# Layer 0's output projection: a third buffer for the cast weights, the squares of h one unit later, gating split at the group change, the last two heads tile by tile

## The chip, the cores and the metric

The kernel runs on one core of a Trainium2 chip. The metric is the device time of one execution in microseconds (us). A profile is one further execution, recorded by the hardware; its rows name engine, source line (L952 is line 952 of the kernel), operation and tiles. The engines are PE (matrix products and transposes), DVE (vector), ACT (scalar functions and casts), POOL (GpSimd) and SP, whose queue issues nearly all transfers between HBM and SBUF. Each engine works through its own queue in order, and waits there for semaphores of the others.

## What is computed

A backbone of two layers over 512 latent and 256 context tokens of width 1024. Layer 0 is a gated DeltaNet in both directions with 16 value heads; layer 1 is grouped-query attention. What matters here is the end of layer 0 and the norm at the start of layer 1:

```python
def finish(o, z):                      # layer 0
    b, h, l, dv = o.shape
    o = rms_norm(jnp.transpose(o, (0, 2, 1, 3)), o_norm_g).astype(z.dtype)
    return (o.reshape(b, l, DN_VAL_DIM) * jax.nn.silu(z)) @ w_out
...
h_lat = h_lat + gate[:, None] * y_lat
h_ctx = h_ctx + gate_c * y_ctx
...
u_lat = rms_norm(h_lat, norm_g[i]) * (1.0 + scale[:, None]) + shift[:, None]   # layer 1
u_ctx = rms_norm(h_ctx, norm_g[i]) * (1.0 + scale_c) + shift_c
```

So the output projection multiplies a 768 x 2048 matrix by w_out (2048 x 1024); its result is gated and added to h, whose rows are then normalised, scaled and shifted for layer 1.

## The kernel before

**Products in float32 by halves.** Each factor is split into a rounded high part and the rest (fp32r each), and a product is three passes over PE: high x high, high x low, low x high (`PASS`, L1009). A weight row block of a head is loaded as `wo` (L942, three buffers), cast to its high part `woh` on ACT (`out_high`, L948 to L953, two buffers), and its low part `wol` is made half on POOL, half on DVE (`out_low`, L955 to L964, two buffers). The activations' halves `y` are made the same way (`out_second`, L1000 to L1007): cast on ACT (L1005), low part on DVE (L1006).

**Units.** The six token tiles lie in two groups of three (`GROUPS`, L970): first the two context tiles 0 and 1 and the latent tile 5, then the tiles 4, 3 and 2. A unit is one head of one group; units 0 to 15 are group 0, units 16 to 31 group 1. The loop over units n starts at L1340. In it stand, in this order:

- the loads of unit n+3 on SP's queue (`out_z`, `out_load`), and at some units loads of h, the gates or layer 1's key and value weights (`w1kv`, L1387, which share the three buffers of `wo`);
- `out_first(n + 2)`: three transposes on PE (L993) and three products with z on DVE (L996);
- from unit 24 on `u_first` (L1307): two transposes (L1312) of the normalised context tiles, scaled and shifted on DVE (L1314), for layer 1. Transposes of both kinds share a PSUM tile with two buffers (`ptr`, tag `tr`);
- `out_second(n + 2)` and `out_high(n + 2)`;
- from unit 24 on `u_second` (L1317): the halves `uC`, cast on ACT (L1320), low part on DVE (L1321);
- `chores`: small pieces of reciprocal square roots on DVE, which use a free part of unit n+2's PSUM tile; `norm_pieces(0)`, the norm of the first group's h, starts at unit 19;
- `out_low(n + 2)`;
- at units 21, 22 and 23 `normed` on ACT (L1301), one tile of the first group each;
- `products0(n)`: 18 products on PE, six for each of the three tiles (L1018), into six PSUM banks (`acc`) that sum over the 16 heads;
- after unit 15 and after unit 31 `gated` (L1243): six products of the banks with the gate on DVE (L1250), into the tiles `gy` in SBUF;
- at units 16, 17 and 18 two calls of `added` (L1254): the sum h + gy on POOL (L1257), the square of h with its row sum on ACT (L1258), and, for latent tiles, the write-out of h on SP's queue (L1260). For group 1 the six calls come after the loop, with the sum on DVE.

The order of PE, DVE, ACT and POOL is as written (`manual_schedule`, L1329); that of SP's queue is worked out by the scheduler. What writes a buffer waits until the last reader of the tile that had it before is done.

After the loop PE does the key and value products of the context tiles (`kv_block(k, (0, 1))`, L1516), while DVE makes the norm of group 1 (`norms1`, L1518) and ACT and DVE scale its tiles (`normed`, L1520); then the latent tiles are transposed and multiplied (L1522 to L1536).

Of the kernel before, what the change touches and what calls it, by code (L numbers as in the profile page):

```python
# [8 lines left out]
F32 = mybir.dt.float32  # L9
F32R = mybir.dt.float32r  # L10
I32 = mybir.dt.int32
AF = mybir.ActivationFunctionType
# [5 lines left out]
P = 128  # L18
D = 1024
# [4 lines left out]
QH, VH = 8, 16  # L24
# [73 lines left out]
def backbone(tc, a, out):  # L98
    nc = tc.nc
    V, S, G, T = nc.vector, nc.scalar, nc.gpsimd, nc.tensor  # L100
# [838 lines left out]
    def out_load(n):  # L939

        gi, h = units0[n]
        w = fw.tile([P, D], F32, tag="w", name=f"wo{h}_{gi}", bufs=3)  # L942
        w_at[n] = dma(w, a["dn_w_out"][0, h * P:(h + 1) * P, :]).ins
        loaded[n] = w
# [3 lines left out]
    def out_high(n):  # L948

        gi, h = units0[n]  # L950
        wh = fw.tile([P, D], F32R, tag="wh", name=f"woh{h}_{gi}")
        S.copy(wh, loaded[n])  # L952
        halves_w[n] = wh  # L953

# [12 lines left out]
    fw = fw_c.__enter__()  # L967


    GROUPS = (((0, 0, 192), (1, 64, 64), (5, 256, 64)), ((4, 128, 64), (3, 64, 192), (2, 0, 320)))  # L970
    ZCOLS = (((0, 256), (NCTX + 192, 128)), ((NCTX, 192), (NCTX + 320, 192)))
    units0 = [(gi, h) for gi in range(2) for h in range(VH)]
    ys, weights, zs, w_at, loaded = {}, {}, {}, {}, {}

    def out_z(n):

        gi, h = units0[n]
        z = fw.tile([P, 3 * P], F32, tag="z", name=f"z{h}_{gi}", bufs=3)
        c = 0
        for c0, m in ZCOLS[gi]:  # L980
            dma(z[:, c:c + m], z_d[h, :, c0:c0 + m])
            c += m
        zs[n] = z
# [3 lines left out]
    def out_first(n):  # L987

        gi, h = units0[n]
        z = zs.pop(n)  # L990
        pt = ptr.tile([P, 4, P], F32, tag="tr", name=f"pt{h}_{gi}")
        for j, (t, off, st_) in enumerate(GROUPS[gi]):
            T.transpose(pt[:, j, :], O[t][:, h, :], ident)  # L993
        for j, (t, off, st_) in enumerate(GROUPS[gi]):
            pj = pt[:, j].rearrange("p (a k) -> p a k", a=2)
            V.scalar_tensor_tensor(pj, pj, og, raw(z, off, [[st_, 2], [1, 64]]), ALU.mult, ALU.mult)  # L996
        begun[n] = pt
        return pt
# [12 lines left out]
    def products0(n, acc, js):  # L1011

        gi, h = units0[n]
        y, ww = ys[n], weights[n]
        for j in js:
            for nh in range(2):
                for x, (i, k) in enumerate(PASS):
                    T.matmul(acc[j][nh], y[i][:, j, :], ww[k][:, nh * 512:(nh + 1) * 512], start=h == 0 and x == 0, stop=h == VH - 1 and x == 2)  # L1018
# [6 lines left out]
    def first_acc(gi):  # L1025

        x = pU.tile([P, 2, 512], F32, tag="su", name=f"po{gi}0")
        return [x[:, nh] for nh in range(2)]

    with tc.tile_pool(name="psC", bufs=2, space=PSUM, reuse_waits="tile") as pcx:  # L1030
# [152 lines left out]
        chores = [(24, scale_pieces(0, 2)), (39, scale_pieces(5, 1))]  # L1183
# [40 lines left out]
    hpool = hpool_c.__enter__()  # L1224
    h_t = [hpool.tile([P, D], F32, tag=f"h{t}", name=f"h{t}") for t in range(NT)]
# [5 lines left out]
    hsq = hpool.tile([P, NT, 2], F32, tag="hsq", name="hsq")  # L1231
# [8 lines left out]

    ORDER = [t for g_ in GROUPS for t, _, _ in g_]

    def gated(gi, acc):  # L1243

        out_ = []
        for j, (t, _, _) in enumerate(GROUPS[gi]):
            for nh in range(2):
                gy = hpool.tile([P, 512], F32, tag="gy", name=f"gy{t}_{nh}", bufs=6)
                c = slice(nh * 512, (nh + 1) * 512)
                V.tensor_tensor(gy, acc[j][nh], gate0[:, 1 if t < 2 else 0, c], ALU.mult)  # L1250
                out_.append((t, nh, gy))
        return out_

    def added(t, nh, gy, E):  # L1254

        c = slice(nh * 512, (nh + 1) * 512)
        E.tensor_tensor(h_t[t][:, c], h_t[t][:, c], gy, ALU.add)  # L1257
        S.activation(gy, h_t[t][:, c], AF.Square, accum_out=hsq[:, ORDER.index(t), nh:nh + 1])  # L1258
        if t >= 2 and nh == 1:
            dma(h_d[t - 2], h_t[t])  # L1260

# [16 lines left out]
    def norm_pieces(gi):  # L1278

        r = hr[:, 3 * gi:3 * gi + 3]  # L1280
        y = hpool.tile([P, 3], F32, tag="hy", name=f"hy{gi}")
        sp = (yield)[:, 0:3]
        V.tensor_copy(sp, hsq[:, 3 * gi:3 * gi + 3, 0])
        V.tensor_tensor(sp, sp, hsq[:, 3 * gi:3 * gi + 3, 1], ALU.add)
        V.tensor_scalar(sp, sp, 1.0 / D, EPS, ALU.mult, ALU.add)
        V.tensor_copy(r, sp)
        V.tensor_single_scalar(sp.bitcast(I32), sp.bitcast(I32), 1, ALU.logical_shift_right)
        V.tensor_scalar(y.bitcast(I32), sp.bitcast(I32), -1.0, float(0x5F3759DF), ALU.mult, ALU.add)
        for i in range(3):
            room_ = yield  # L1290
            sp, t_ = room_[:, 0:3], room_[:, 64:67]
            V.tensor_copy(sp, y)
            V.scalar_tensor_tensor(t_, sp, -0.5, y, ALU.mult, ALU.mult)
            V.tensor_tensor(t_, t_, r, ALU.mult)
            V.scalar_tensor_tensor(r if i == 2 else y, t_, 1.5, y, ALU.add, ALU.mult)

    def normed(t, E):

        r = hr[:, ORDER.index(t):ORDER.index(t) + 1]
        if E is S:  # L1300
            S.activation(h_t[t], h_t[t], AF.Copy, scale=r)  # L1301
        else:
            E.tensor_scalar(h_t[t], h_t[t], r, None, ALU.mult)
# [3 lines left out]
    def u_first(k, j, tiles):  # L1307

        n = len(tiles) * P
        ps = ptr.tile([P, 4, P], F32, tag="tr", name=f"ht{k}_{j}")  # L1310
        for q, t in enumerate(tiles):
            T.transpose(ps[:, q, :], h_t[t][:, k * P:(k + 1) * P], ident)  # L1312
        pv = ps.rearrange("p a b -> p (a b)")[:, 0:n]
        V.tensor_scalar(pv, pv, au[1][:, j, 1, k:k + 1], au[1][:, j, 0, k:k + 1], ALU.mult, ALU.add)  # L1314
        turned_u[k, j] = pv
# [17 lines left out]
    chores = {4: scale_pieces(4, 1), 7: scale_pieces(3, 1), 10: scale_pieces(2, 1)}  # L1333
    for g_ in chores.values():
        next(g_)
    chores[19] = norm_pieces(0)
    squares = [(t, h) for t in (4, 3, 2) for h in range(VH)]
    late_adds = []
    loads0 = {3: lambda: load_h(0), 5: lambda: load_h(1), 7: lambda: load_h(5), 9: lambda: dma(gate0[:, 0], gate_d[0][:, 0]), 11: lambda: dma(gate0[:, 1], gate_d[0][:, 1]), 13: lambda: load_h(4), 18: lambda: load_h(3), 20: lambda: load_h(2)}
    for n in range(len(units0)):  # L1340
        gi, h = units0[n]
        if h == 0:
            acc = [acc0 if gi == 0 else first_acc(1)] + [[pf.tile([P, 512], F32, tag=f"po{j}{nh}", name=f"po{gi}{j}{nh}") for nh in range(2)] for j in (1, 2)]
        if n + 3 < len(units0):
            out_z(n + 3)
            out_load(n + 3)
        if n in loads0:
            with tc.issue_after(w_at[n + 3]):
                loads0[n]()
        more = n + 2 < len(units0)  # L1350
        pt = out_first(n + 2) if more else None
        if n >= 24:
            u_first(n - 24, 1, (0, 1))
        if more:
            out_second(n + 2)
            out_high(n + 2)
        if n >= 24:
            u_second(n - 24, 1, uC)
        if n == 19:
            next(chores[19])  # L1360
        for x in [x for x in chores if x <= n]:
            for _ in range(2):
                try:
                    chores[x].send(pt[:, 3])
                except StopIteration:
                    chores.pop(x)
                    break
        if more:
            out_low(n + 2)
        for t, h_ in squares[:5]:  # L1370
            square_o(t, h_)
        squares = squares[5:]
        scale_o(2 if n >= 12 else 1)
        if n in (21, 22, 23):
            normed(ORDER[n - 21], S)
        products0(n, acc, (1, 2) if n < 2 else (0, 1, 2))
        if h == VH - 1:
            late_adds = gated(gi, acc)
        if n in (16, 17, 18):
            for x in range(2):  # L1380
                added(*late_adds.pop(0), G)
        if gi == 1 and h in (4, 6, 8, 10):
            S.copy(wkv[0][:, k0:k0 + 2], wv)
            G.tensor_tensor(wkv[1][:, k0:k0 + 2], wv, wkv[0][:, k0:k0 + 2], ALU.subtract)
        if gi == 1 and h in (3, 5, 7, 9):
            k0 = h - 3
            w = fw.tile([P, D], F32, tag="w", name=f"w1kv_{k0}", bufs=3)  # L1387
            wv = w.rearrange("p (k n) -> p k n", n=512)
            dma(wv, wa[:, k0:k0 + 2, 1024:1536])
    for t, nh, gy in late_adds:  # L1390
        added(t, nh, gy, V)
    opool_x = [fw_c, opool_c, gates_c]
    for p_ in opool_x:
        p_.__exit__(None, None, None)
# [400 lines left out]
    with tc.tile_pool(name="fo", bufs=2, side="right", reuse_waits="tile") as f2, tc.tile_pool(name="psO", bufs=1, space=PSUM, reuse_waits="tile") as pO:  # L1795
# [4 lines left out]
        acc = [pg]  # L1800
# [4 lines left out]
        for t in range(4):  # L1805
            hs = f2.tile([P, D], F32, tag="hs", name=f"hs{t}")
            dma(hs, h_d[t])
            jk = f2.tile([P, D], F32, tag="jko", name=f"jko{t}")
# [3 lines left out]
            for nh in range(2):  # L1812
                c = slice(nh * 512, nh * 512 + 512)
# [11 lines left out]
            for hf in range(2):  # L1825
                c = t if hf == 0 else 7 - t
# [35 lines left out]
```

## Time and profile before

| | us |
|---|---|
| median of 3 runs | 1247.38 (1246.32 to 1249.12) |
| the profiled execution | 1246.04 |
| its span in the profile | 1244.3 |
| PE busy | 1151.5 (93%) |
| DVE, ACT, POOL busy | 827.8, 724.5, 599.3 |
| L1018, the projection's products, first to last start | 778.2 to 940.9 |

The profile is a page of sums and a trace of single instructions. A row of the trace's timeline has the start in us from the span's start, the busy time, the engine, the line, the operation with output and input tiles, a count, and in brackets the idle time of the engine before it and what ended that. A row of the waits has who waited for whom, the total in us, how often and the longest. A row of the windows has the busy time of each engine in a stretch, the share of its full clock that PE was granted (1.00 is full speed), and how busy the 16 DMA engines were. Products on PE are pipelined: the next starts before the one before it ends, so starts tell the rate.

### The profile page before, as it was taken

Reading aid. Unit: us, or ns where it says so; the run is one execution under the profiler, and the core shown is the slowest. Engines: PE = TensorE matmul, PEld = TensorE weight load, DVE = VectorE, ACT = ScalarE, POOL = GpSimd, SP = SyncE. Lnnn points to the kernel's source line nnn. Section 1 sums busy time; section 2 is a strip of 40 time slices with the busy share of each in tenths; the row PEclk is TensorE's granted clock in tenths of the full one; section 3 lists DMA queues with packets and bytes.
Section 4 is the critical chain, followed back from the end, with each engine's and each line's share of the span. In section 5 each row is a group of like instructions: output and inputs, shape, how many; then the busy total and the mean of one; then the engine's idle time right before and its main releaser. Section 6 shows DMA issues by size and latency. Waiting matters only on the chain. (4 is left out here: it accounts for less than half of the span.)

```text
span 1244.3 us, 28131 instructions
## 1 busy us (share of the span) xinstructions
PE 1151.5 (93%) x10755; PEld 926.9 (74%) x10755; DVE 827.8 (67%) x1865; ACT 724.5 (58%) x1934; POOL 599.3 (48%) x486
## 2 busy tenths in 40 slices
PE   4999999999789979899999999999879889999896
PEld 1776778888678867788666666887667779989784
DVE  2497666768688555575688988675556766556545
ACT  5543336665575767974689897543523246666631
POOL 0121133159998999700485598456534043140540
PEclk9999999999899989899999999999999999999998
DMA  9578965556425588655979765675634012111133
GB/s 322 176 216 263 299 221 162 137 151 183 136 83 159 181 253 261 191 193 184 274 215 241 237 172 143 199 224 153 213 103 136 18 41 62 35 34 52 51 110 93
DMA packets 165496, 204.56 MB, mean 164 GB/s; under 512 B 13393, under 2 KB 114930, under 8 KB 164594
## 3 DMA queue, kind: packets, MB, share of 16 engines
q1 hardware_dynamic: 146162, 193.10, 51.0%
q10 hardware_dynamic: 19200, 9.67, 2.6%
q8 instruction: 85, 1.39, 0.5%
q14 instruction: 49, 0.40, 0.1%
HBM read 161.96 MB, written 40.67 MB: 163 GB/s over the span
## 5 line engine op out<-in xcount | busy, mean ns | idle before, releaser
L1113 POOL TENSOR_TENSOR S<-S,glb 128x512 f32<-128x512 f32 x88 | 90.0, 1045 | 109.4 <-PE ks L1105 109.4
L1018 PE MATMUL po<-woh,y 128*128 128x512 f32 x384 | 128.7, 403 | 2.9 <-DVE gy L1250 2.9
L414 PE MATMUL g_v<-uh,wh 128*128 128x512 f32 (+1 forms) x256 | 91.4, 357 | 15.0 <-DVE sil_v L441 15.0
L755 POOL TENSOR_TENSOR X<-X,tmp 128x62 f32<-128x62 f32 (+15 forms) x93 | 95.7, 1029 | 6.5
L436 DVE SCALAR_TENSOR_TENSOR acc_v<-g_v,cwv,acc_v 128x510 f32<-128x510 f32 (+3 forms) x128 | 74.5, 609 | 34.5 <-ACT acc_v L433 33.0
L414 PE MATMUL g_z<-uh,wh 128*128 128x512 f32 (+1 forms) x256 | 88.4, 345 | 7.7 <-DVE sil_v L441 7.7
L1105 PE MATMUL ks<-S,ckq 128*64 128x256 f32 x768 | 93.5, 385 | 0.7 <-ACT O L1110 0.6
L754 POOL TENSOR_TENSOR tmp<-L,X 128x62 f32<-128x62 f32 (+15 forms) x93 | 89.9, 966 | 6.9
L414 PE MATMUL g_v<-ul,wh 128*128 128x512 f32 (+1 forms) x256 | 89.5, 350 | 0.0
L414 PE MATMUL g_v<-uh,wl 128*128 128x512 f32 (+1 forms) x256 | 88.9, 347 | 0.0
L961 POOL TENSOR_TENSOR wol<-wo,woh 128x512 fp32r<-128x512 f32 (+1 forms) x32 | 50.3, 1572 | 77.3 <-ACT woh L952 59.0
L414 PE MATMUL g_z<-ul,wh 128*128 128x512 f32 (+1 forms) x256 | 86.9, 340 | 0.0
L414 PE MATMUL g_z<-uh,wl 128*128 128x512 f32 (+1 forms) x256 | 86.9, 340 | 0.0
L1018 PEld LDWEIGHTS po<-woh,y 128*128 128x128 f32 x384 | 72.9, 190 | 18.2 <-issue 3.2
L1105 PEld LDWEIGHTS ks<-S,ckq 128*64 128x64 f32 x768 | 50.7, 136 | 39.7 <-ACT O L1110 9.9
L1018 PE MATMUL po<-wol,y 128*128 128x512 f32 x192 | 75.9, 396 | 1.5 <-POOL wol L961 1.4
L414 PEld LDWEIGHTS g_v<-uh,wh 128*128 128x128 f32 x256 | 50.6, 198 | 21.7 <-DVE sil_v L441 15.8
L211 POOL TENSOR_TENSOR wl_k<-w_k,wh_k 128x1024 fp32r<-128x1024 f32 x8 | 19.2, 2400 | 98.7 <-ACT wh_k L210 98.7
L1658 DVE TENSOR_TENSOR pT<-pt,pT 128x384 fp32r<-128x384 f32 x64 | 33.3, 554 | 42.2 <-ACT pT L1657 42.2
L1178 DVE TENSOR_TENSOR S<-su,S 128x512 f32<-128x512 f32 x88 | 56.6, 685 | 5.0 <-PE su L1160 3.4
L1108 DVE SCALAR_TENSOR_TENSOR r<-ks,negV,cv 128x128 f32<-128x128 f32 x192 | 56.6, 344 | 4.3 <-PE ks L1105 3.5
L414 PEld LDWEIGHTS g_z<-uh,wh 128*128 128x128 f32 x256 | 48.8, 191 | 13.6 <-DVE sil_v L441 8.5
(410 smaller groups left out, 3376.8 us busy)
## 6 DMA issues: line engine op xcount, KB each, us to landing
aw<-in_ada_w SPq DMA_DIRECT2D x24, 1024.0 KB, 7.8
w<-in_dn_w_in SPq DMA_DIRECT2D x40, 512.0 KB, 4.3
wo<-in_dn_w_out SPq DMA_DIRECT2D x32, 512.0 KB, 3.7
cv<-v_d SPq DMA_DIRECT2D x80, 128.0 KB, 5.5
df<-gc_d SPq DMA_DIRECT2D x48, 128.0 KB, 2.9
z_d<-zs SPq DMA_DIRECT2D x16, 384.0 KB, 4.9
v_d<-vt ACTq DMA_DIRECT2D x16, 384.0 KB, 3.8
t_d<-Tt SPq DMA_DIRECT2D x6, 1024.0 KB, 5.1
```

The source lines that it names most:

```text
L211: split_at[0] = E.tensor_tensor(wl[:, :, :m], w[:, :, :m], wh[:, :, :m], ALU.subtract).ins
L414: mm = T.matmul(pg_[:m, :n], w[:, k, :m], u[:, k, c0:c0 + n], start=k == 0 and n_ == 0, stop=k == KT - 1 and n_ == 2)
L436: V.scalar_tensor_tensor(acc[:, c0 + lo:c0 + hi], ps[:, lo + j - 2:hi + j - 2], cwv[:, j, ct:ct + 1], acc[:, c0 + lo:c0 + hi], ALU.mult, A ...
L754: E.tensor_tensor(tv, bcast(L[:, :, j + 1:, j], 3, j + 1), bcast(X[:, :, j, 0:j + 1], 2, n), ALU.mult)
L755: E.tensor_tensor(X[:, :, j + 1:, 0:j + 1], X[:, :, j + 1:, 0:j + 1], tv, ALU.subtract)
L961: G.tensor_tensor(wl[:, :c], w[:, :c], wh[:, :c], ALU.subtract)
L1018: T.matmul(acc[j][nh], y[i][:, j, :], ww[k][:, nh * 512:(nh + 1) * 512], start=h == 0 and x == 0, stop=h == VH - 1 and x == 2)
L1105: T.matmul(ks[r0:r0 + 64, w], kq[:, w, slot(hh), r0:r0 + 64], St[hh][:, d], start=True, stop=True)
L1108: V.scalar_tensor_tensor(r[:, 2 * j + i], ks[:, 0, i], negV[:, visit, t, h0 + i:h0 + i + 1], v[:, 2 * hh + i], ALU.mult, ALU.add)
L1113: G.tensor_tensor(St[hh], St[hh], bcast(g_, 3, P), ALU.mult)
L1178: V.tensor_tensor(St[hh], raw(sj, 0, [[512 - 1024 * j, 2], [P, 2], [1, P]]), St[hh], ALU.add)
L1658: V.tensor_tensor(lo, ps[:, :3], hi, ALU.subtract)
```

## The change

Four things in the loop over the units:

1. `woh` gets a third buffer (`bufs=3`).
2. At units 16 to 18 the squares of h are no longer issued with the sums; each pair is issued one unit later, on ACT behind that unit's casts of y and of the weights. The write-out of tile 5 goes with its square. `norm_pieces(0)` starts at unit 20 and `normed` runs at units 22, 23 and 24, one later than before.
3. At unit 15 the products are issued ahead of `out_second`, and the gating products of the first two tiles right behind them; those of the third tile follow `out_second` and `out_high`, ahead of `out_low`.
4. Units 30 and 31 are multiplied tile by tile: both heads of the first tile in unit 30, both heads of the second and then of the third tile in unit 31. The second group's gating writes its product in place, into the PSUM banks, and each tile is gated, added and squared before the next.

```diff
@@ out_high
-        wh = fw.tile([P, D], F32R, tag="wh", name=f"woh{h}_{gi}")
+        wh = fw.tile([P, D], F32R, tag="wh", name=f"woh{h}_{gi}", bufs=3)
@@ gated
-    def gated(gi, acc):
+    def gated(gi, acc, js):
 
         out_ = []
-        for j, (t, _, _) in enumerate(GROUPS[gi]):
+        for j in js:
+            t = GROUPS[gi][j][0]
             for nh in range(2):
-                gy = hpool.tile([P, 512], F32, tag="gy", name=f"gy{t}_{nh}", bufs=6)
                 c = slice(nh * 512, (nh + 1) * 512)
+                gy = acc[j][nh]
+                if gi == 0:
+                    gy = hpool.tile([P, 512], F32, tag="gy", name=f"gy{t}_{nh}", bufs=6)
                 V.tensor_tensor(gy, acc[j][nh], gate0[:, 1 if t < 2 else 0, c], ALU.mult)
@@ added
         E.tensor_tensor(h_t[t][:, c], h_t[t][:, c], gy, ALU.add)
-        S.activation(gy, h_t[t][:, c], AF.Square, accum_out=hsq[:, ORDER.index(t), nh:nh + 1])
+
+    def square_h(t, nh):
+
+        c = slice(nh * 512, (nh + 1) * 512)
+        jk = hpool.tile([P, 512], F32, tag="gy", name=f"jh{t}_{nh}", bufs=6)
+        S.activation(jk, h_t[t][:, c], AF.Square, accum_out=hsq[:, ORDER.index(t), nh:nh + 1])
         if t >= 2 and nh == 1:
             dma(h_d[t - 2], h_t[t])
@@ before the loop
-    chores[19] = norm_pieces(0)
+    chores[20] = norm_pieces(0)
+    late_squares = []
@@ in the loop
+        if n == VH - 1:
+            products0(n, acc, (0, 1, 2))
+            late_adds = gated(gi, acc, (0, 1))
         if more:
             out_second(n + 2)
             out_high(n + 2)
         if n >= 24:
             u_second(n - 24, 1, uC)
-        if n == 19:
-            next(chores[19])
+        if n == VH - 1:
+            late_adds += gated(gi, acc, (2,))
+        if n == 20:
+            next(chores[20])
...
-        if n in (21, 22, 23):
-            normed(ORDER[n - 21], S)
-        products0(n, acc, (1, 2) if n < 2 else (0, 1, 2))
-        if h == VH - 1:
-            late_adds = gated(gi, acc)
+        for t, nh in late_squares:
+            square_h(t, nh)
+        late_squares = []
+        if n in (22, 23, 24):
+            normed(ORDER[n - 22], S)
+        last = len(units0) - 1
+        if n >= last - 1:
+            for j in ((0,), (1, 2))[n - last + 1]:
+                products0(last - 1, acc, (j,))
+                products0(last, acc, (j,))
+        elif n != VH - 1:
+            products0(n, acc, (1, 2) if n < 2 else (0, 1, 2))
         if n in (16, 17, 18):
             for x in range(2):
+                late_squares.append(late_adds[0][:2])
                 added(*late_adds.pop(0), G)
@@ after the loop
-    for t, nh, gy in late_adds:
-        added(t, nh, gy, V)
+    for j in range(3):
+        for t, nh, gy in gated(1, acc, (j,)):
+            added(t, nh, gy, V)
+            square_h(t, nh)
```

## The prediction, made before the result was known

> **What bounds the kernel now.** I read the page, then the windows cut at the units of layer 0's output projection, then the waits of that stretch, then the timelines of PE, ACT, DVE and POOL around each wait. The page's first row says that PE is busy for 93% of the span: idle time of PE is what an edit here can win.
>
> ```profile
> PE 1151.5 (93%) x10755; PEld 926.9 (74%) x10755; DVE 827.8 (67%) x1865; ACT 724.5 (58%) x1934; POOL 599.3 (48%) x486
> ```
>
> A unit n (one head, three token tiles) is three transposes for unit n+2, from unit 24 on two more for layer 1 (L1312), and 18 products. The windows start where PE starts a unit: 16, 17, 18, 22, 24, 25, 30, then the kv products and the rest. Columns: window, its length, busy time of PE, PEld, DVE, ACT and POOL with counts, granted clock, DMA share, GB/s.
>
> ```profile
> 849.82:858.96 9.14, 6.27 (x22) 4.83 (x21) 5.83 (x11) 1.52 (x2) 2.47 (x2) 0.81 0.45 151
> 858.96:863.43 4.47, 4.47 (x22) 3.66 (x21) 1.68 (x4) 1.06 (x2) 3.10 (x3) 1.00 0.14 26
> 863.43:885.82 22.39, 18.72 (x86) 14.42 (x85) 10.31 (x35) 10.64 (x21) 12.32 (x10) 1.00 0.57 180
> 885.82:894.91 9.09, 9.09 (x44) 7.31 (x43) 6.28 (x15) 6.27 (x8) 7.00 (x5) 1.00 0.88 254
> 894.91:899.71 4.80, 4.80 (x25) 3.85 (x23) 3.05 (x7) 2.58 (x3) 3.50 (x2) 1.00 0.85 252
> 899.71:932.38 32.67, 24.31 (x116) 19.31 (x116) 17.95 (x35) 10.87 (x17) 11.98 (x7) 1.00 0.37 117
> 932.38:941.09 8.71, 8.71 (x41) 7.15 (x40) 6.00 (x11) 2.06 (x4) 1.30 (x1) 1.00 0.00 0
> ```
>
> An undisturbed unit takes 4.47 us (unit 17). Unit 16 takes 9.14, units 18 to 21 take 22.39 for four, units 25 to 29 take 32.67 for five. The rows of the waits from 778 to 980 name the causes (total, times, longest):
>
> ```profile
> ACT woh L952 <- PE po L1018: 19.2, 14, 2.0
> ACT gy L1258 <- POOL h L1257: 11.1, 6, 3.2
> PE ht L1312 <- DVE uC L1321: 8.4, 5, 1.7
> PE po L1018 <- DVE gy L1250: 2.9, 1, 2.9
> PE pt L993 <- DVE hy L1295: 2.1, 1, 2.1
> PE po L1018 <- POOL wol L961: 1.4, 1, 1.4
> ```
>
> **Part 1, third buffer of woh.** With two buffers the copy of unit n+2 on ACT waits until unit n's products have ended. From unit 24 on, uC's copy stands behind it on ACT, and PE's next L1312 transposes wait for uC, because their PSUM tile has two buffers.
>
> ```profile
> 899.95 1.04 ACT L952 CAST woh<-wo 128x1024 fp32r<-128x1024 f32 x1 [1.06 <-PE po L1018]
> 900.90 0.36 ACT L1320 CAST uC<-ht 128x256 fp32r<-128x256 f32 x1
> 901.30 0.42 DVE L1321 TENSOR_TENSOR uC<-ht,uC 128x256 fp32r<-128x256 f32 x1 [1.81 <-ACT uC L1320]
> 901.87 0.41 PE L1312 MATMUL ht<-ident,h 128*128 128x128 f32 x2 [1.67 <-DVE uC L1321]
> 902.04 0.48 PE L1018 MATMUL po<-woh,y 128*128 128x512 f32 x1
> ```
>
> Unit 24's products end when unit 25 starts, at 899.71; then woh 1.04, uC 0.36, its low part 0.42, and the transposes start at 901.87, 2.16 into the unit. With three buffers woh only waits for unit n-1, which is over. What is late next? wol keeps two buffers, so POOL's and DVE's halves still wait for unit n's products; on DVE that wait holds up the next unit's L996, L1314, L1006 and L1321. Their durations:
>
> ```profile
> 842.48 0.69 DVE L963 TENSOR_TENSOR wol<-wo,woh 128x512 fp32r<-128x512 f32 x1 [0.39 <-ACT woh L952]
> 842.53 1.79 POOL L961 TENSOR_TENSOR wol<-wo,woh 128x512 fp32r<-128x512 f32 x1 [0.76 <-ACT woh L952]
> 904.04 0.48 ACT L1005 CAST y<-pt 128x384 fp32r<-128x384 f32 x1 [1.83 <-DVE pt L996]
> 902.82 1.14 DVE L996 SCALAR_TENSOR_TENSOR pt<-pt,og,z 128x128 f32<-128x128 f32 x3
> 903.86 0.55 DVE L1314 TENSOR_SCALAR ht<-ht,au 128x256 f32<-128x256 f32 x1
> 904.55 0.56 DVE L1006 TENSOR_TENSOR y<-pt,y 128x384 fp32r<-128x384 f32 x1
> ```
>
> Let a unit start at T. wol is released 0.24 later (899.95 less 899.71) and takes DVE 0.69: T+0.93. L996 starts then; y's copy starts 1.22 after L996's start (904.04 less 902.82) and takes 0.48: T+2.63. Then woh 1.04, uC 0.36, low part 0.42: T+4.45, and 0.15 to PE (901.87 less 901.72): T+4.60. L1314 and L1006 end at L996's start plus 2.29, so they are covered. The next transposes are due after the rest of the unit and the three transposes of L993, 0.25 (two take 901.87 to 902.04): a unit with L1312 lies between 4.47 and 4.80 (unit 24, with a short wait in it); I take 4.65, so due at T+4.9. It fits by 0.3. Gain of units 25 to 29: 32.67 less 5 x 4.65 = 9.4 us, between 8.7 (4.80) and 10.3 (4.47).
>
> **The lock.** The 0.69 holds only if DVE starts before POOL. Elsewhere the order is the other way:
>
> ```profile
> 806.52 1.30 POOL L961 TENSOR_TENSOR wol<-wo,woh 128x512 fp32r<-128x512 f32 x1 [2.67 <-ACT woh L952]
> 806.54 1.82 DVE L963 TENSOR_TENSOR wol<-wo,woh 128x512 fp32r<-128x512 f32 x1
> ```
>
> Here POOL began 0.02 earlier and DVE's half took 1.82. When DVE stands idle at the release it starts first (842.48 against 842.53). In the forecast DVE is done with uC's low part at T+4.45 and the release is at T+4.65+0.24, so DVE wins. A late uC loses, and then everything is 1.13 later: T+5.73 instead of 4.9, 0.85 a unit. I charge 0.4 in all for half a unit lost. The Trainium skill ("SBUF — State Buffer", two separate sides of SBUF) calls the port pair of DVE and GpSimd an exclusive lock that blocks the loser for a whole instruction; that speaks against this change, which releases both halves in the same moment, and these rows agree (1.30 plus about 0.52). If the loser were always DVE, its sum is the lock rival's below.
>
> **Part 2, squares a unit later.** L1258 sits on ACT ahead of the next unit's y and waits for POOL's add, which waits behind wol.
>
> ```profile
> 862.09 2.54 POOL L1257 TENSOR_TENSOR h<-h,gy 128x512 f32<-128x512 f32 x2
> 863.42 0.63 ACT L1258 ACTIVATE gy<-h 128x512 f32<-128x512 f32 x1 [3.16 <-POOL h L1257]
> 865.29 0.46 ACT L1005 CAST y<-pt 128x384 fp32r<-128x384 f32 x1
> ```
>
> y's copy comes at 865.29, after both squares; three units of this make wol (1.40) and the norm pieces on DVE (2.06) late for PE. A unit later the squares stand behind y and woh, and POOL has finished: wol to T+0.24+1.79, two adds 2.54, so T+4.57; squares end at most 1.87 later (863.42 to 865.29 for two, with a wait between), T+6.44, which is 1.97 into the next unit, before the y copy due at 0.93+1.22 = 2.15 there. Gain of units 18 to 21: 22.39 less 4 x 4.47 = 4.5. The write-out of h's tile 5 moves along on SP's queue; its data are ready 4.57 into unit 19, and the weight loads behind it need wol's end 2 us into unit 20, so it costs nothing; what stands behind the three write-outs at the end serves products after the kv stage. norm_pieces and normed move one unit on. normed of the second context tile is now in unit 23, right before the transposes that read it: y ends at T+2.63, woh at 3.67, normed 1.1 (half of the row 2.21 below) gives T+4.8, against 4.47+0.25: 0.1 late, up to 1 if ACT is held by a wkv copy. I take 0.4.
>
> **Part 3, group change.** All six gating products stand behind wol on DVE and after unit 15's last product, and unit 16 needs their PSUM.
>
> ```profile
> 851.75 3.67 DVE L1250 TENSOR_TENSOR gy<-po,gate 128x512 f32<-128x512 f32 x6
> 853.17 0.62 PE L1018 MATMUL po<-woh,y 128*128 128x512 f32 x1 [2.87 <-DVE gy L1250]
> L1018 PE MATMUL po<-woh,y x206: 387/393/628, 844.7 to 940.9; 128*128 128x512 f32 x103
> ```
>
> Now four of them run while unit 15's later tiles are multiplied (0.61 each; two per 1.4 us of products), and the last two (1.2 us) end about 1 us into unit 16, whose third tile starts after 0.25 plus 12 of 18 products, near 3. Queued behind them on DVE are y's low part of unit 17, its wol and unit 18's L996; wol of unit 17 can then end about 2 us into unit 16 and is needed at its end. Gain 9.14 less 4.47 = 4.67: 2.87 idle, and 1.8 because the products after it are slow (one 0.62 where the median is 0.39, granted clock 0.81). By the Trainium skill ("TensorE: Matmul & The Clock Gate", Part 1) the clock falls only after an idle window of about 3.4 us; then the slow products were not the wait's doing, this term is 2.87, and the sum is 1.8 smaller. The clock row decides for me: 1.00 in the windows around it. No shorter wait (2.06, 1.67) lowers it: their windows have 1.00.
>
> **Part 4, last two heads by tile.** PE's work is the same. Unit 31's first tile now wants wol early: released 0.24 into unit 30, 1.30 to 1.79 on POOL, so 1.5 to 2.0; PE comes there after two transposes and seven products of about 0.24 (8.71 over 36), near 1.9. Cost 0 to 0.15; I take 0.1. At the end:
>
> ```profile
> 942.15 3.69 DVE L1257 TENSOR_TENSOR h<-h,gy 128x512 f32<-128x512 f32 x6
> 950.03 2.21 ACT L1301 ACTIVATE h<-h,hr 128x1024 f32<-128x1024 f32 x2 [3.37 <-DVE hr L182]
> 941.09 11.09 PE L1449 MATMUL kv<-wkv,uC 128*128 128x512 f32 x48
> 952.29 1.09 PE L1312 MATMUL ht<-ident,h 128*128 128x128 f32 x8
> ```
>
> gating, adds, squares, norm and normed end at 952.24, the kv products that cover them at 952.18. Two tiles of three are now added while PE multiplies the others, so after the last product DVE has some 2 x 0.61 of gating and 2 x 0.61 of adding instead of six adds behind six gatings; the chain ends about 1.5 earlier. PE gains 0.1, since its kv products end last. Gating in place in PSUM is not in the trace: below is 0.61 (a gating into SBUF), above 0.82:
>
> ```profile
> 952.99 0.82 DVE L1314 TENSOR_SCALAR ht<-ht,au 128x512 f32<-128x512 f32 x1 [1.63 <-PE ht L1312]
> ```
>
> I take 0.7: 0.1 more for six, within the 1.5. At 0.82 it is 1.3, still covered.
>
> **Sum.** 9.4 + 4.5 + 4.7 + 0.1 - 0.4 (lock) - 0.4 (normed) - 0.1 (unit 31) = 17.8 us. The profiled execution took 1246.04 (span 1244.3), giving 1228.2; the median of the runs is 1247.38, 1.3 higher, giving **1229.6 us**.
>
> **Rivals.** *Lock lost* (0.17): DVE stays behind POOL from unit 25 on, 5 x 0.85 = 4.3 us, less the 0.4 charged: 13.9 gained, 1233.5. For it: the two halves start within 0.05 us. Against: DVE is idle 0.4 us before the release.
>
> *Loads late* (0.08): shared with the kv loads, w's three buffers give a weight load only two units from unit 23 on. It is issued after POOL's half, T+2.03; the row of wo's issues from 860 to 935 says when it lands:
>
> ```profile
> DMA to landing us min/median/max: 3.2/3.4/4.9
> ```
>
> So 3.4 later, at worst 4.9: T+5.4 to 6.9, that is 0.8 to 2.3 into the next unit, where woh wants it at 2.63. Units 18 to 23 must move in 26.8 us what took 31.5 at shares 0.57 and 0.88, so 0.77 on average. At a landing of 6.5 woh is 1.25 late in each of units 24 to 27, less the 0.3 that fits: 3.8 us, 1233.4.
>
> *Part 3 does not do what it says* (0.03): the last two gatings still hold unit 16, 4.7 less: 1234.3.
>
> *Slower than before* (0.03): the same loads, but landing so late that units 24 to 28 each idle 2.87 us and then run slowly, as unit 16 did: 5 x 4.67 = 23.4 less 17.8, 5.6 slower, 1253.0. It decides from a landing of 2.87+0.3+2.63+4.65-2.03 = 8.4 us on; the slowest seen is 4.9, at a DMA share of up to 0.88.
>
> No change at all needs several of these together: 0.02. More gained than 19.5 (0.03) would need idle time that I don't see.
>
> **How the numbers follow.** The forecast has 0.64: its own range is 17 to 19.5 off, 1228 to 1231. The range reaches to the lock and load rivals above, with the 1.7 us by which the slowest run stands over the median and a little for both at once (1236.0), and to 20.3 off the fastest run below (1226.0; part 1 at its upper bound is 0.9 more). About 0.2% (2.5 us) is what a measurement of this kernel can tell from none. Faster 0.95, same 0.02, slower 0.03.
>
> **What would show it.** Unit 16 near 4.5 us with clock 1.00; units 18 to 21 near 17.9; units 25 to 29 near 23.3; woh's wait for po gone, DVE's wol now waiting for po instead; L1250 before L1006 at the group change; kv products ending last. Wrong if the L1312 transposes still wait for uC by 0.8 each (lock or loads: DVE's wol at 1.8, or woh behind a DMA), or if what is won there comes back as waits after the kv products.

## The result and the profile after

| | before | after |
|---|---|---|
| median of 5 runs, us | 1247.38 (1244.33 to 1249.12) | 1226.71 (1224.16 to 1228.17) |
| ratio, 95% interval | | 0.9834 (0.9813 to 0.9854) |
| the profiled execution, us | 1246.04 | 1227.47 |
| its span, us | 1244.3 | 1225.7 |

The change makes the kernel 1.7% faster. The forecast was 1229.6 us, in a range of 1226.0 to 1236.0. The profiled execution is 18.57 us shorter and the medians are 20.67 apart; the forecast for both was 17.8.

The page of the kernel after: PE's totals, and the two groups of products whose idle time was the target. Before, the last column read 2.9 and 1.5.

```profile
PE 1147.3 (94%) x10755; PEld 925.9 (76%) x10755; DVE 828.0 (68%) x1865; ACT 724.0 (59%) x1934; POOL 600.7 (49%) x486
...
L1018 PE MATMUL po<-woh,y 128*128 128x512 f32 x384 | 127.7, 400 | 0.0
...
L1018 PE MATMUL po<-wol,y 128*128 128x512 f32 x192 | 75.0, 391 | 0.0
```

PE executes the same 10755 instructions; 4.2 us of its busy time have gone too, 1.8 of them in unit 16 (6.27 to 4.47), whose products ran at a low clock before.

The windows of the kernel after, cut at the same units as before: 16, 17, 18 to 21, 22 and 23, 24, 25 to 29, 30 and 31.

```profile
851.82:856.29 4.47, 4.47 (x23) 3.66 (x22) 3.74 (x8) 1.11 (x2) 1.29 (x1) 1.00 0.44 131
856.29:860.76 4.47, 4.47 (x23) 3.66 (x22) 2.23 (x5) 2.37 (x5) 4.02 (x3) 1.00 0.51 162
860.76:878.63 17.87, 17.87 (x86) 14.65 (x85) 11.59 (x32) 9.97 (x19) 14.81 (x10) 1.00 0.87 258
878.63:887.56 8.93, 8.93 (x44) 7.32 (x43) 5.63 (x17) 5.79 (x8) 5.31 (x3) 1.00 0.71 209
887.56:892.23 4.67, 4.67 (x25) 3.88 (x24) 3.11 (x7) 2.85 (x6) 1.98 (x2) 1.00 0.76 222
892.23:915.56 23.33, 23.33 (x117) 19.40 (x116) 15.60 (x35) 10.55 (x18) 13.31 (x7) 1.00 0.49 156
915.56:924.45 8.89, 8.89 (x42) 7.07 (x41) 6.35 (x12) 2.08 (x6) 1.72 (x1) 1.00 0.05 19
```

In every row the second and third number are equal: PE is busy from the first to the last unit, and the granted clock is 1.00 throughout. Unit 16 fell from 9.14 to 4.47, units 18 to 21 from 22.39 to 17.87, units 25 to 29 from 32.67 to 23.33.

The waits of the kernel after from 778 to 965. PE's own waits for uC, gy, hy and wol, 14.8 us before, are not among them.

```profile
DVE wol L963 <- PE po L1018: 7.5, 10, 1.4
...
PE ht L1320 <- DVE uL L1329: 3.0, 3, 2.0
...
PE ht L1320 <- DVE ksq L182: 2.7, 1, 2.7
```

DVE's half of wol now waits for PE, where woh did before: the bound in the units has gone over to PE. PE's own waits come after them, among the latent columns of layer 1 (uL, and the norm of the context's keys, ksq).

One unit from unit 25 on, in the timeline of the kernel after. A unit starts at 896.88 and the next at 901.55.

```profile
898.77 0.48 ACT L1005 CAST y<-pt 128x384 fp32r<-128x384 f32 x1 [2.55 <-DVE pt L996]
...
899.15 1.05 ACT L952 CAST woh<-wo 128x1024 fp32r<-128x1024 f32 x1
...
900.10 0.37 ACT L1328 CAST uC<-ht 128x256 fp32r<-128x256 f32 x1
...
900.50 0.43 DVE L1329 TENSOR_TENSOR uC<-ht,uC 128x256 fp32r<-128x256 f32 x1 [0.66 <-ACT uC L1328]
...
901.58 0.69 DVE L963 TENSOR_TENSOR wol<-wo,woh 128x512 fp32r<-128x512 f32 x1 [0.65 <-PE po L1018]
901.71 1.72 POOL L961 TENSOR_TENSOR wol<-wo,woh 128x512 fp32r<-128x512 f32 x1 [2.95 <-ACT wkv L1405]
...
901.88 0.38 PE L1320 MATMUL ht<-ident,h 128*128 128x128 f32 x2
```

woh no longer waits (no bracket). uC's low part ends at 900.93, 0.95 before the transposes that need its PSUM tile; DVE is idle for 0.65 when wol is released, starts 0.13 ahead of POOL, and takes 0.69.

The group change, on DVE in the kernel after:

```profile
849.27 2.48 DVE L1253 TENSOR_TENSOR gy<-po,gate 128x512 f32<-128x512 f32 x4
851.67 0.55 DVE L1006 TENSOR_TENSOR y<-pt,y 128x384 fp32r<-128x384 f32 x1
852.14 1.27 DVE L1253 TENSOR_TENSOR gy<-po,gate 128x512 f32<-128x512 f32 x2
853.33 0.68 DVE L963 TENSOR_TENSOR wol<-wo,woh 128x512 fp32r<-128x512 f32 x1
```

Four gatings end 0.1 before unit 16 starts (851.82), the last two 1.6 into it.

Of the 18.57 us, stage by stage of the two traces (positive is shorter after): unit 16 4.67, units 18 to 21 4.52, units 22 and 23 0.16, unit 24 0.13, units 25 to 29 9.34, units 30 and 31 -0.18, key and value products of the context 0.26, of the latents 1.6, and -2.0 ahead of unit 0, which starts at 781.73 in place of 779.72 although no part is aimed at what comes before it. Together 18.5.

### The profile page after: what moved, and what is told of

Read it like the earlier page. It is cut to its first block, busy times and chain, and to the rows that moved or that the text cites. A ratio compares the mean times of both kernels' runs of the same rounds, so it can differ in the third digit from the quotient of the medians.

```text
span 1225.7 us, 28180 instructions
## 1 busy us (share of the span) xinstructions
PE 1147.3 (94%) x10755; PEld 925.9 (76%) x10755; DVE 828.0 (68%) x1865; ACT 724.0 (59%) x1934; POOL 600.7 (49%) x486
## 4 chain that ended last, share of the span: by engine, by line
PE 65%; DVE 11%; POOL 9%; DMA 6%; ACT 6%; issue 3%; SPq 1%; ACTq 0%; DVEq 0%; POOLq 0%
PE po L1018 11%; PE ks L1105 7%; PE g_z L414 6%; PE g_k L414 4%; PE g_q L414 4%; POOL X L755 4%; POOL tmp L754 3%; PE pg L1590 3%; PE su L1160 3%; PE kv L1473 3%; PE po L1699 2%; PE pr L1130 2%; PE pso L1718 2%; PE pa L245 2%; PE pg L1636 2%
```

## The experiments

All ratios are against the kernel before, run on the same chip beside it: medians 1245.61 (25 runs), 1246.96 (15 runs) and 1246.72 (9 runs) for the three sets that follow. This table gives the length of each stage in us, from the starts of PE's instructions in each trace; the first column is the start of unit 0, and the last runs from the first transposes of the latents to the end of their key and value products.

| kernel | start | 16 | 18–21 | 22–23 | 24 | 25–31 | latents |
|---|---|---|---|---|---|---|---|
| before | 779.7 | 9.15 | 22.38 | 9.09 | 4.80 | 41.38 | 36.08 |
| after | 781.7 | 4.47 | 17.87 | 8.93 | 4.67 | 32.22 | 34.47 |
| p1_alone | 782.9 | 6.38 | 21.88 | 9.15 | 5.20 | 33.79 | 36.75 |
| p2_alone | 781.3 | 9.16 | 17.85 | 8.93 | 6.68 | 41.29 | 36.10 |
| p3_alone | 781.5 | 4.47 | 22.48 | 9.04 | 4.84 | 41.30 | 36.07 |
| p4_alone | 781.2 | 10.39 | 23.98 | 8.91 | 4.67 | 42.33 | 35.30 |
| uc_first | 779.4 | 9.15 | 22.38 | 9.08 | 4.87 | 32.02 | 32.95 |
| no_p1 | 778.6 | 4.47 | 17.87 | 8.93 | 6.68 | 42.25 | 32.89 |
| no_p4 | 781.7 | 4.47 | 17.87 | 8.93 | 4.67 | 32.02 | 34.50 |
| kvnorm_late | 782.2 | 4.47 | 17.87 | 8.93 | 4.67 | 32.19 | 30.97 |
| two_buf_order | 781.2 | 4.47 | 17.87 | 8.93 | 6.68 | 33.52 | 36.74 |
| after_again | 783.1 | 4.47 | 17.87 | 8.93 | 4.67 | 32.19 | 36.05 |
| kvnorm_again | 784.0 | 4.47 | 17.87 | 8.93 | 4.67 | 32.22 | 32.51 |

My theory: each of parts 1 to 3 takes away one wait of PE, their gains add up, and part 4 is worth about nothing. The rivals: part 1 loses much of its gain to the lock on DVE or to late loads; part 1 is only a cure for the order of ACT's queue.

### One part at a time

**Part 1 alone.**

```diff
-        wh = fw.tile([P, D], F32R, tag="wh", name=f"woh{h}_{gi}")
+        wh = fw.tile([P, D], F32R, tag="wh", name=f"woh{h}_{gi}", bufs=3)
```

> The kernel before with the third buffer of woh and nothing else. Theory (each wait has a part of its own): units 25 to 29 fall from 32.67 us to 23.3, units 18 to 21 stay at 22.4 and unit 16 near 9.1; the time falls by 9.4 us (ratio 0.9925). Rival (the three waits have one root, ACT held by woh's wait for the products): units 18 to 21 fall to about 18 too, 14 us in all (0.989).

Measured: 1237.52 us, 0.9938 (0.9917 to 0.9959). PE's waits in its trace, and then the end of unit 24 and unit 25, where the lock is lost:

```profile
PE po L1018 <- DVE gy L1250: 1.7, 1, 1.7
...
PE ht L1312 <- DVE uC L1321: 0.6, 1, 0.6
```

```profile
895.84 1.05 ACT L952 CAST woh<-wo 128x1024 fp32r<-128x1024 f32 x1 [1.14 <-DMA wo<-in_dn_w_out]
...
900.40 1.28 POOL L961 TENSOR_TENSOR wol<-wo,woh 128x512 fp32r<-128x512 f32 x1 [1.58 <-ACT woh L952]
900.57 0.43 DVE L1321 TENSOR_TENSOR uC<-ht,uC 128x256 fp32r<-128x256 f32 x1 [0.66 <-ACT uC L1320]
...
900.91 1.32 DVE L963 TENSOR_TENSOR wol<-wo,woh 128x512 fp32r<-128x512 f32 x1
...
901.15 0.41 PE L1312 MATMUL ht<-ident,h 128*128 128x128 f32 x2 [0.57 <-DVE uC L1321]
```

The waits for uC went from 8.4 us to 0.6, and units 18 to 21 kept 21.88 us, so the waits don't have one root. Here the prediction's two rivals come in together, and small: woh waited 1.14 for a load, so uC came late, POOL took the lock 0.51 ahead, and DVE's half took 1.32 instead of 0.69. In the units after, POOL starts 0.07 to 0.24 ahead and DVE's half takes 1.59 to 1.76. Units 25 to 28 took 5.44, 4.84, 4.97 and 4.87 where 4.67 is undisturbed: 0.77 once and then 0.2 to 0.3 a unit. In the full change woh waits for no load there, nor in no_p4 below, so part 4 isn't needed for that; whether part 2 or 3 brings it was not tried apart. Another 1.4 us is lost far behind the units, where PE's order is another one (see no_p4). An effect that I had not foreseen: part 1 also shortens unit 16, to 6.38. wol and the gating had stood behind woh's 1.04 us cast, and without it PE waits 1.7 instead of 2.9, and its products afterwards are not slow.

**Part 2 alone.**

```diff
@@ added
-        S.activation(gy, h_t[t][:, c], AF.Square, accum_out=...)
@@ in the loop
+        for t, nh in late_squares:
+            square_h(t, nh)
-        if n in (21, 22, 23):
-            normed(ORDER[n - 21], S)
+        if n in (22, 23, 24):
+            normed(ORDER[n - 22], S)
```

> The kernel before with the squares of h one unit later, and the norm and the scaling of the first group one unit on, nothing else. Theory: units 18 to 21 fall from 22.39 us to 17.9, units 25 to 29 stay at 32.7, unit 16 near 9.1; 4.5 us less (0.9964). Rival (one root): with woh still waiting on ACT, the later squares only move the wait, and units 18 to 22 keep at least 2 of the 4.5 us (0.998 or more).

Measured: 1242.0 us, 0.9962 (0.9943 to 0.998). PE's waits:

```profile
PE ht L1317 <- DVE uC L1326: 8.4, 5, 1.7
...
PE ht L1317 <- ACT h L1306: 1.8, 1, 1.8
```

Units 18 to 21 take 17.85, as forecast. But unit 24 takes 6.68: with two buffers of woh, the later `normed` stands on ACT behind a woh that waits for PE, and the transposes wait 1.8 for it. Part 2 pays 1.9 of its 4.5 us back unless part 1 is there.

**Part 3 alone.**

```diff
+        if n == VH - 1:
+            products0(n, acc, (0, 1, 2))
+            late_adds = gated(gi, acc, (0, 1))
         if more:
             out_second(n + 2)
             out_high(n + 2)
...
+        if n == VH - 1:
+            late_adds += gated(gi, acc, (2,))
...
```

> The kernel before with the gating of group 0 split around unit 15's later products, nothing else. Theory (the idle time lowers the clock): unit 16 falls from 9.14 us to 4.5 with the granted clock at 1.00, 4.7 us less (0.9963). Rival (the slow products come from something else): the idle 2.87 goes, but some products of unit 16 or 17 still run at half speed, 2.9 us less (0.9977). The other units stay as before in both.

Measured: 1242.96 us, 0.9975 (0.9962 to 0.9988). The ratio can't tell the theory from its rival, since 0.9963 and 0.9977 both lie in the interval; the trace can. Unit 16 takes 4.47 instead of 9.15 with the granted clock at 1.00, and nothing else moves by more than 0.1 in the units.

**Part 4 alone.**

```diff
+        if n >= last - 1:
+            for j in ((0,), (1, 2))[n - last + 1]:
+                products0(last - 1, acc, (j,))
+                products0(last, acc, (j,))
...
+    for j in range(3):
+        for t, nh, gy in gated(1, acc, (j,)):
+            added(t, nh, gy, V)
...
```

> The kernel before with units 30 and 31 tile by tile and the second group gated in place, nothing else. Theory: PE's kv products end last either way, so units 30 and 31 and the kv products take 19.8 to 20.0 us instead of 19.91, and the time stays within 0.2 us (0.9998 to 1.0002 but for noise). Rival (the gating and norm chain sets the end): the chain ends 1.5 us earlier and the time falls by as much (0.9988).

Measured: 1245.43 us, 0.9995 (0.9983 to 1.0006): no difference. Two rows of its windows, unit 16 and units 18 to 21, none of which part 4 touches:

```profile
851.30:861.70 10.40, 7.53 (x22) 5.75 (x21) 5.82 (x11) 1.52 (x2) 2.50 (x2) 0.67 0.39 134
...
866.20:890.20 24.00, 20.36 (x86) 15.69 (x85) 11.83 (x38) 10.62 (x21) 13.93 (x10) 0.93 0.61 185
```

Beside the same rows of before (9.14 at a clock of 0.81, 22.39 at 1.00) they show the same idle time followed by more time at a low clock. What part 4 does itself: units 30 and 31 cost 1.0 more, because unit 31's wol, behind a waiting woh, is 0.7 late for the first tile; the context's products gain 0.3.

### Order or buffer

**uc_first.** The kernel before, with uC's copy ahead of woh's cast on ACT and still two buffers.

```diff
             out_second(n + 2)
-            out_high(n + 2)
         if n >= 24:
             u_second(n - 24, 1, uC)
+        if more:
+            out_high(n + 2)
```

> The kernel before with two buffers of woh, and on ACT and DVE the halves of uC ahead of the cast of woh, nothing else. Theory (what cost units 25 to 29 was only that uC stood behind woh's wait on ACT): units 25 to 31 fall from 41.4 us to 32.5 to 34.5 without a third buffer, while ACT still waits as long for the products before each woh; unit 16 and units 18 to 21 stay at 9.1 and 22.4; 7 to 9 us less (0.993 to 0.9945). Rival (the wait for the products itself, through wol, POOL and DVE): units 25 to 31 stay above 38.

Measured: 1234.97 us, 0.9906 (0.9873 to 0.9939), better than expected. PE's waits, in which uC doesn't occur, neither here nor in the rows left out:

```profile
PE ht L1312 <- DVE uL L1321: 3.0, 3, 2.0
PE po L1018 <- DVE gy L1250: 2.9, 1, 2.9
PE ht L1312 <- DVE ksq L182: 2.7, 1, 2.7
...
```

Units 25 to 31 take 32.02, as short as with the third buffer (32.22), although ACT still waits for PE before woh there (5.7 us, 10.9 before). For these units the fault was the order on ACT: a copy that PE needed soon stood behind one that waited for PE. The rest of the gain in this trace, 3.1 us among the latents, is clock (below).

**no_p1.** The change without the third buffer.

```diff
-        wh = fw.tile([P, D], F32R, tag="wh", name=f"woh{h}_{gi}", bufs=3)
+        wh = fw.tile([P, D], F32R, tag="wh", name=f"woh{h}_{gi}")
```

> The changed kernel with two buffers of woh again. Theory: units 25 to 31 go back from 32.2 us to 41.4, and unit 24 to 6.7 as in the run of part 2 alone, because normed of the second context tile stands behind a woh that waits; units 16 to 21 stay at 4.47 each; 11 us slower than the changed kernel, 0.992 of the kernel before. Rival (parts 2 and 3 need the third buffer): units 16 to 21 lose 2 us or more of their gain as well.

Measured: 1240.6 us, 0.9948 (0.9929 to 0.9966). PE's waits:

```profile
PE ht L1320 <- DVE uC L1329: 8.4, 5, 1.7
...
PE ht L1320 <- ACT h L1309: 1.8, 1, 1.8
...
PE po L1018 <- POOL wol L961: 0.7, 1, 0.7
```

Against the change, unit 24 costs 2.0 more and units 25 to 31 10.0 more, and the median is 13.9 higher where 11 was expected; 1.4 of this is another order of PE far behind (see no_p4). Two of these waits are not in the kernel before: parts 2 and 4 lean on the third buffer as well.

**two_buf_order.** The change with two buffers and uc_first's order.

```diff
-        wh = fw.tile([P, D], F32R, tag="wh", name=f"woh{h}_{gi}", bufs=3)
+        wh = fw.tile([P, D], F32R, tag="wh", name=f"woh{h}_{gi}")
...
-            out_high(n + 2)
         if n >= 24:
             u_second(n - 24, 1, uC)
+        if more:
+            out_high(n + 2)
```

> The changed kernel with two buffers of cast weights instead of three, and ScalarE's copy of the turned context (uC) put ahead of the weight cast (woh) in units 24 to 31. If it was the order on ScalarE that cost the 1.9 us a unit and the third buffer only hid it, units 25 to 31 take about 32.0 us here as in uc_first, against 32.2 with three buffers and 42 in no_p1, and the time stands at 0.983 to 0.986 of the kernel before. If parts 2 and 4 need the third buffer by themselves, unit 24 costs 1.8 to 2.0 us more (the normalised h behind a waiting weight cast) and unit 31 up to 1.0 us more: 0.985 to 0.987. If the third buffer is needed whatever the order, 0.993 to 0.995 as in no_p1.

Measured: 1232.25 us, 0.9883 (0.9859 to 0.9906), between the second of the three cases and the third. Two of PE's waits:

```profile
PE ht L1320 <- ACT h L1309: 1.8, 1, 1.8
PE po L1018 <- POOL wol L961: 1.2, 1, 1.2
```

Units 25 to 29 take 23.37: the order is enough for them. Unit 24 costs 2.0 and units 30 and 31 1.3 more, as the second case had it. So 3.3 us of the 5.8 by which its median stands over after_again's lie in the units. The two traces are 2.1 us apart in span (1230.8 and 1228.7): these 3.3, 0.7 more among the latents, and a start 1.9 earlier. The other 2.5 us of the medians I can't place.

### Part 4, and what is left after the change

**no_p4.** The change without part 4.

```diff
-        last = len(units0) - 1
-        if n >= last - 1:
-            ...
-        elif n != VH - 1:
+        if n != VH - 1:
             products0(n, acc, (1, 2) if n < 2 else (0, 1, 2))
...
```

> The changed kernel with the last two heads unit by unit and the second group gated into SBUF after them, as before. Theory: units 30 and 31 take 8.71 us instead of 8.89, the kv products 11.2 instead of 10.94, the rest is the same; within 0.3 us of the changed kernel, 0.983 to 0.985 of the kernel before. Rival (the norm's chain ends last now that PE is earlier): the latent transposes start 1 us or more later.

Measured: 1229.48 us (1227.02 to 1231.27), 0.9858 (0.9828 to 0.9888). In its units and in the context's products the sum differs from the change by less than 0.1 us (32.02 and 11.17, against 32.22 and 10.94), so part 4 does nothing on PE. The medians differ by 2.8 us with overlapping intervals. In the profiled execution 1.4 lies far behind (257.25 us from the end of the latents' products to the end of the kernel, in place of 255.83), and the trace shows where: about 205 us behind those products, in layer 1's attention, PE executes its instructions in another order than in the change, with ten products that wait for pT (0.75 and 0.21 us) ahead of the ones that fill this time there. The traces of no_p1 and p1_alone have this order and the same 1.4; the other traces have neither. No edit stands in that part; why these three programs got another order there is not known. The 257.09 of kvnorm_again is something else: its extra time lies 23 to 33 us behind the products, where a half-clock stretch falls at another place. I put neither down to what part 4 does.

**kvnorm_late.** The change, with the norm of the context's keys behind the third block of the latents instead of the second, so that PE need not wait for it (the 2.7 us of ksq).

```diff
-        if k == 1:
+        if k == 2:
             kv_norm((0, 1), "c")
             kv_values((0, 1))
-        if k in (2, 3):
-            k_turned(k - 2)
-            rope_by(1, k - 2)
+        if k == 3:
+            for i in range(2):
+                k_turned(i)
+            for i in range(2):
+                rope_by(1, i)
```

> The changed kernel with the norm of the context keys one step later in the kv stage (behind the seventh block of the latent transposes instead of the fifth) and the turned context keys and their tables behind the eighth. Theory (PE's idle 2.69 us there is the norm's 16 small operations on DVE ahead of the next block, and it brings the slow clock after it): the stretch from the first latent transposes to the last kv product falls from 34.47 us to 30 to 31.5, 3 to 4.5 us faster than the changed kernel, 0.980 to 0.981 of the kernel before. Rival (the same operations hold up the eighth block or the keys' transposes instead): the stretch stays above 33.

> The version with the context's norm moved behind the third block of latent columns, unaltered, for an interval beside the changed kernel on one chip. If the PE wait on the norm's squares (2.7 us) was on the path, it lies 2.0 to 3.5 us below the changed kernel (0.9802 to 0.982 of the kernel before); if the first reading of 1224.4 was chance, within 1 us of it.

> The changed kernel unaltered, on the same chip as the two beside it. 0.982 to 0.985. Its PE stages up to the end of unit 31 should repeat within 0.3 us; the stage of the latent keys and values (34.47 us in the first profile) should read either about 34.5 or about 33.0, by whether a window of half clock falls into it: if it reads anything else, the clock isn't what the 1.6 us came from.

Measured: kvnorm_late 1224.42 us, 0.9825 (0.9795 to 0.9854); again 1224.19 us, 0.9821 (0.9793 to 0.985); the change beside it, after_again, 1226.43 us, 0.9834 (0.9812 to 0.9856). PE's waits in the first of them from 780 to 965, in which ksq is gone:

```profile
PE ht L1320 <- DVE uL L1329: 3.3, 4, 2.0
PE pq L1152 <- DVE O L1163: 0.5, 1, 0.5
```

The medians of all runs, 1224.42 of nine against 1226.57 of ten, are 2.2 us apart, less than the 3 to 4.5 expected first, within the 2.0 to 3.5 expected of the second, and less than the intervals of the ratios can tell. The traces tell it: the latents stage is 30.97 and 32.51 us with the edit, against 34.47 and 36.05 without, and 1.9 to 2.0 of that stays when traces with equally many half-clock stretches are compared (next paragraph). It is the best version that I have.

The other half of after_again's expectation fell: the stage read 36.05, neither 34.5 nor 33.0. I had written that another value would speak against the clock. It doesn't, because I had not thought of two half-clock stretches in one stage. Windows of before (two), after (one) and after_again (two) follow, cut at these stretches, and then two of uc_first; the column before the last two is the granted clock.

```profile
955.73:959.14 3.41, 3.41 (x11) 2.74 (x10) 2.11 (x4) 1.17 (x2) 1.59 (x2) 0.50 0.33 99
969.39:972.80 3.41, 3.41 (x10) 2.66 (x9) 2.10 (x4) 1.17 (x2) 0.00 (x0) 0.50 0.00 0
```

```profile
950.80:954.21 3.41, 3.41 (x10) 2.63 (x9) 2.10 (x4) 1.17 (x2) 0.00 (x0) 0.50 0.41 138
```

```profile
939.92:943.33 3.41, 3.41 (x11) 2.82 (x11) 2.10 (x4) 1.18 (x2) 1.04 (x1) 0.50 0.73 217
953.58:956.99 3.41, 3.41 (x10) 2.66 (x9) 2.10 (x4) 1.17 (x2) 0.00 (x0) 0.50 0.00 0
```

```profile
950.00:955.00 5.00, 3.87 (x20) 2.77 (x18) 3.24 (x9) 2.75 (x12) 3.42 (x2) 1.00 0.40 121
955.00:960.00 5.00, 2.73 (x14) 2.33 (x15) 3.97 (x16) 0.59 (x1) 0.00 (x0) 1.00 0.27 89
```

uc_first (and no_p1) have none and take 32.9; after and no_p4 have one and take 34.5; before and after_again have two and take 36.1. So a half-clock stretch costs about 1.6 us, and without one the stage would take 32.9 in before and after alike. The 1.6 us that the change seemed to win there is one stretch fewer in that execution; after_again gives it back, and with a start 1.4 later it accounts for the 3.0 us by which its span (1228.7) exceeds the first.

## Why the prediction was right

- **Part 1** (9.4): 9.34 in units 25 to 29. The wait that goes and the step that is late next were right. The margin was larger than worked out: uC's low part ends 4.05 into the unit (900.93 less 896.88), not 4.45. Two things were mis-sized: wol starts 0.03 into the unit, not 0.24, and a step starts about 0.1 before the one ahead of it on its engine has ended its busy time (y to woh 0.38 for a busy time of 0.48, woh to uC 0.95 for 1.05), so that a chain of busy times is too long.
- **The lock** (charge 0.4, rival 0.17): in units 25 to 29 of the change DVE starts first each time (0.69), so nothing fell due. The rival's mechanism exists (p1_alone), but its price there is 0.2 to 0.3 a unit after the first, not 0.85. DVE's half does lose 0.9 to 1.1 there (1.59 to 1.76 for 0.69), near the 1.13 of the prediction; what it put too low is the margin that covers this, 0.95 from the end of uC's low part to the transposes in the change's rows, where 4.9 less 4.45 is 0.45. The Trainium skill ("SBUF — State Buffer", two separate sides of SBUF) has the loser of the port wait for a whole instruction; the rows of p1_alone agree (0.69 alone, 1.32 behind POOL).
- **Late loads** (0.08): seen once, 1.14 us on woh in p1_alone; not in the change.
- **Part 2** (4.5): 4.52. The charge of 0.4 for `normed` did not fall due: unit 24 took 4.67. I had costed it at a y that ends 2.63 into the unit; without part 1 it costs 1.9 (p2_alone), a dependence that the prediction does not mention.
- **Part 3** (4.7): 4.67, and the clock with it: 1.00 in unit 16. The Trainium skill ("TensorE: Matmul & The Clock Gate", Part 1) puts the fall of the clock after at least one idle window of about 3.4 us, by which this term was 2.87 and the sum 1.8 smaller. The runs speak against that threshold: unit 16 was slow after 2.87 idle in all four traces that have this wait at its full length (9.15 to 10.39 in before, p2_alone, p4_alone and uc_first, against 4.47 and 2.87 together), and not without the wait. But the prediction also read that shorter waits don't lower the clock, and that isn't so: in p4_alone a wait of 2.04 for hy did (0.93 in units 18 to 21). The 1.8 of this term was read off one execution, and its size hangs on where the wait falls (last section), which the prediction didn't know.
- **Part 4** (0.1 gained, 0.1 lost): 0.26 gained, 0.18 lost, and no_p4 confirms that it is nothing. The gating in place took 0.69 where 0.7 was assumed.
- **The sum.** Of 18.57, the terms give 18.9 (with 0.16 of units 22 and 23, which I had not forecast). The rest, +1.6 and -2.0, is clock and start, at neither of which the change is aimed: that they nearly cancel is chance. The start is open: the six traces with a third buffer start unit 0 at 781.7 to 784.0 and the seven with two at 778.6 to 781.5, but the two traces of the change itself already differ by 1.4 there, and the medians show no such loss. What made the forecast the smaller one against these stages is the 0.8 of charges for the lock and `normed`. The medians' 20.67 lies beyond 19.5, to which the prediction gave 0.03; the interval of the ratio reaches from 18.2 to 23.3 us and holds the stages' 18.9, and what more the medians show is not explained.

## What to carry to other kernels

When an engine's queue holds a copy that waits for PE, look at what stands behind it: the 1.9 us a unit here were lost by an unrelated copy, and either a third buffer or a swap of two lines wins them. A buffer also covers later edits that an order alone doesn't (3.3 us here), so measure parts alone and left out, since a part's worth depends on the others. And before a microsecond or two in a stage that was not edited is explained, read its granted clock, and see whether PE's order there is still the same (1.4 us here).

## What was unexpected of the hardware

PE runs at half clock in whole periods of 3.41 us. The kept traces record each change of the granted clock, and in each of the 13 these changes lie on one grid of that length, and the grid lies elsewhere in each trace. These windows are cut at the grid; the third number is PE's busy time, the one before the last two the granted clock. First comes unit 16 of before, then the same wait in p4_alone:

```profile
849.92:853.33 3.41, 0.54 (x5) 0.33 (x4) 2.19 (x4) 1.04 (x1) 2.37 (x2) 1.00 0.51 187
853.33:856.74 3.41, 3.41 (x9) 2.64 (x9) 3.08 (x7) 0.18 (x1) 0.00 (x0) 0.50 0.47 159
```

```profile
850.57:853.98 3.41, 1.26 (x8) 0.81 (x6) 1.86 (x4) 1.04 (x1) 2.74 (x3) 1.00 0.64 211
853.98:857.39 3.41, 2.70 (x7) 2.15 (x7) 3.38 (x7) 0.00 (x0) 0.49 (x1) 0.50 0.44 154
857.39:860.80 3.41, 3.41 (x9) 2.64 (x8) 1.12 (x3) 0.48 (x1) 0.00 (x0) 0.50 0.22 62
```

In before the whole wait of 2.87 us lies in one period, and the next one runs at half clock. In p4_alone a boundary cuts it: PE is busy for 1.26 of the first period, the next one is at half clock and holds the rest of the wait, and the one after that is at half clock too. So unit 16 takes 10.39 there against 9.15. The wait of 2.69 us for ksq shows the same, in after and then in no_p1:

```profile
947.39:950.80 3.41, 0.81 (x6) 0.77 (x7) 3.00 (x16) 0.00 (x0) 1.81 (x1) 1.00 0.61 170
```

```profile
953.59:957.00 3.41, 1.88 (x10) 1.10 (x8) 2.24 (x9) 2.16 (x11) 3.31 (x2) 1.00 0.34 96
957.00:960.41 3.41, 1.52 (x9) 1.35 (x10) 2.91 (x13) 0.16 (x1) 0.00 (x0) 1.00 0.67 214
```

In after all but 0.1 of it (947.30 to 949.99) lies in one period, and the period at 950.80, shown above, is at half clock. In no_p1 it is cut in two, and the clock stays at 1.00. In all periods of the 13 traces from 300 us on, a full-clock period with PE busy for at most 1.5 us was followed by half clock, and one with 1.65 us or more never was; between them both occur. After a half-clock period with up to 2.8 us busy came another one, from 2.9 on full clock. So the same wait costs its length and then nothing, 1.6 to 1.8 or 3 us, by where it falls on the grid. What sets the grid's place no run here shows.
